# The sample's weighted expert rows: one DVE operation, or a scaling on ACT and an addition on POOL, in a hybrid decoder step

## The chip, the cores and the metric

The kernel runs on one core of a Trainium2 chip. A core has several engines that work side by side, each in the order of its own queue: TensorE (PE, matrix products; its weight loads are listed as PEld), VectorE (DVE), ScalarE (ACT) and GpSimd (POOL). SyncE (SP) and the other queues issue DMA transfers. The metric is the device time of one execution in microseconds (us), as the median of several runs. The kernel before has a median of 2448.68 us in three runs (2442.91 to 2449.34).

## The reference

The program is one inference step of a one-layer decoder, for a prompt of 512 tokens and for a sample group of 8 sequences of 8 tokens. Both go through a combined projection, a retention branch, a dilated-attention branch and a PEER block, with layer norms between. The PEER block is the part that matters here. It has 16,384 experts, each a row of two tables, `u_tab` and `v_tab`, of 1024 numbers. For each token and each of 8 heads it picks 16 experts by product keys and adds their rows up:

```python
def block(xb):
    q = (xb @ w_q).reshape(PEER_BLOCK, H_PEER, 2, DK_PEER // 2)
    s = jnp.einsum('thsc,hskc->thsk', q, sub_keys).astype(jnp.float32)
    sv, si = lax.top_k(s, TOPK_PEER)
    cand = (sv[:, :, 0, :, None] + sv[:, :, 1, None, :]).reshape(PEER_BLOCK, H_PEER, TOPK_PEER * TOPK_PEER)
    cv, ci = lax.top_k(cand, TOPK_PEER)
    i0 = jnp.take_along_axis(si[:, :, 0], ci // TOPK_PEER, axis=-1)
    i1 = jnp.take_along_axis(si[:, :, 1], ci % TOPK_PEER, axis=-1)
    e = i0 * N_KEYS + i1
    g = jax.nn.softmax(cv, axis=-1)
    a = jax.nn.gelu(jnp.einsum('td,thkd->thk', xb, u_tab[e]), approximate=False)
    return jnp.einsum('thk,thkd->td', (g * a).astype(xb.dtype), v_tab[e])
```

The last line is a weighted sum of rows. For the sample's 64 tokens the kernel computes it row by row.

## The kernel before, in words

All operations are emitted by one long function. A scheduler then orders the instructions of each engine by a simulation of the timeline, so the order in the code sets priorities and dependences, and not the order on an engine.

**The sample's experts.** The sample's 64 tokens lie twice on the 128 partitions, so that each partition sums half of a token's 128 experts: 64 steps. A step gathers one row of a table per partition into the tile `row` (128x1024 fp32) by an indirect DMA that POOL issues (`gather`, L1112); `row` has four buffers. `experts` first takes 64 rows of the u table (`dot`, L1121: a product with the token and its sum, on DVE), and then 64 rows of the v table (`add`). Of the v rows the first is multiplied by its weight (L1128); each of the others is one DVE operation that multiplies the row by its weight, a column of `a`, and adds it to the sum `ys` (L1130). `advance(n, after)` paces this: it first emits the operations of the rows that were asked for before (`consume`), then makes POOL copy one element of a tile named by `after` (L1144, tile `pace`), and lets n gathers follow that copy. So rows are asked for where the program around has got to a certain tile.

**The stage around the change.** By now 26 of the 64 v rows have been gathered. The prompt's routing begins, in four parts:

- *The scores.* For each of four column groups c, the projections by `w_q` run on PE, in eight accumulations per group, 32 in all, and ACT moves each from PSUM to the tile `qT` (L1463). `advance(GQ, ...)` with GQ = 4 stands twice in each group: eight requests of four rows, 32 rows. Then PE multiplies with the keys, ACT moves the scores to `sc` (L1470, three buffers), and DVE picks the 16 best of each 128 by maxima, index searches and replacements (`top16`, L991 to L999). Weights are split into a high and a low part: ACT copies (`whi`, L315), DVE subtracts (`wlo`, L316).
- *The head of the u-parts.* `u_ahead(HEAD)` runs 16 blocks of the dense expert product (`u_part`): ACT copies the weight (L1434), POOL subtracts for the low part (L1435), PE runs 24 matmuls into `tr` (L423 to L425), and ACT applies Gelu into `act` (L1440).
- *The spread.* `spread(t)`, for three tiles of 128 tokens. `route` combines the two key lists on DVE: candidate sums `cand` (L1013, L1015), their `top16`, a subtraction `ce` (L1030) whose exponential is taken by ACT (L1031), two chains of `eq` that pick the indices (to L1040), and the weights `gw` (L1044). PE transposes the indices and the weights (L1490) and ACT moves them to `tT` (L1492). Then 32 groups of four tokens each follow: one-hot matrices from DVE (`oh1` L1501, `oh0` L1511), ACT (L1507, L1508) and POOL (L1511), products of the two on PE (L1512), and ACT moves them to `stage` (L1513). After every fourth group stand one further `u_part` and `advance(GX, ...)` with GX = 1: six of the v rows fall here.
- *The rest.* The routing of the fourth tile, and 12 or so further u-parts before the main loop.

The main loop runs 128 blocks of the dense experts over some 840 us. In it the sample's result is finished and the fourth prompt tile goes through `experts` too, with 128 rows of each table.

Of the kernel before, what the change touches and what calls it, by code (L numbers as in the profile page):

```python
# [13 lines left out]
AF = mybir.ActivationFunctionType  # L14
OP = mybir.AluOpType
# [209 lines left out]
def body(tc, I, O, dbg=None):  # L225
    nc = tc.nc
    PE, DVE, ACT, POOL, SP = nc.tensor, nc.vector, nc.scalar, nc.gpsimd, nc.sync
# [9 lines left out]
    def pool(name, side=None, space=None):  # L237
        kw = {"reuse_waits": "tile"} if space is None else {"space": space}
        if side:
            kw["side"] = side  # L240
        return tc.alloc_tile_pool(name=name, bufs=1, **kw)
# [20 lines left out]
    def ac_ps():  # L262
        return psum("ac", 3)
# [106 lines left out]
    raws, units, state = [], [], {"done": 0, "bank": ac_ps, "ada": None}  # L370
# [38 lines left out]
    def take(name, c, u, n=2):  # L409

        a = state["done"]
        while len(units) < len(order) and sum(not plain(i) for i in range(a, len(units))) < UB:
            load_units()
            if len(units) == len(raws):
                break
            split_unit()
        load_units()
        assert order[a:a + n] == [(name, c, u + i) for i in range(n)] and len(units) >= a + n, (order[a], name, c, u)
        state["done"] += n
        return units[a:a + n]  # L420
# [120 lines left out]
    def proj_t(w, m, x, ks=range(8), sel=slice(0, L)):  # L541

        ps = mm_ps()[:, 0:sel.stop - sel.start]
        for k in ks:
            mm3(ps, both(w, k, slice(128 * m, 128 * m + 128)), x(k, sel), k == ks[0], k == ks[-1])
        return ps
# [441 lines left out]
    def top16(xs, vs, ixs):  # L988

        for x, v, ix in zip(xs, vs, ixs):  # L990
            DVE.max(v[:, 0:8], x)  # L991
        for x, v, ix in zip(xs, vs, ixs):
            DVE.max_index(ix[:, 0:8], v[:, 0:8], x)
        for x, v, ix in zip(xs, vs, ixs):
            DVE.match_replace(x, v[:, 0:8], x, MINF)
        for x, v, ix in zip(xs, vs, ixs):
            DVE.max(v[:, 8:16], x)
        for x, v, ix in zip(xs, vs, ixs):
            DVE.max_index(ix[:, 8:16], v[:, 8:16], x)  # L999
# [70 lines left out]
    def values(g):  # L1070
        v = two_blocks() + two_blocks()
        for half in range(2):
            w = take("w_av", g, 2 * half)
            cs = slice(256 * half, 256 * half + 256)
            for c in range(4):
                ACT.activation(v[c][:, cs], proj_n(w, h, tiles[c]), AF.Copy)  # L1076
        return v
# [22 lines left out]
    ys = S2.tile([128, D], F32, name="ys", tag="ys")  # L1100

    pending = []

    def consume():
        with tc.issue_after(state["split"]):
            for f in pending:
                f()
        pending.clear()

    def gather(table, e, j):  # L1110
        r = S2.tile([128, D], F32, name="row", tag="row", bufs=ROWS)
        POOL.indirect_dma_start(out=r, out_offset=None, in_=I[table], in_offset=bass.IndirectOffsetOnAxis(ap=e[:, j:j + 1], axis=0))  # L1112
        return r

    def experts(n, e, g, h2, y):

        a = S2.tile([128, 128], F32, name="acts", tag="acts", bufs=1)
        DVE.memset(a, 0.0)

        def dot(u, j):  # L1120
            DVE.scalar_tensor_tensor(u, u, 1.0, h2, op0=OP.mult, op1=OP.mult, accum_out=a[:, j:j + 1])  # L1121
            if j == n - 1:
                ACT.activation(a[:, 0:n], a[:, 0:n], AF.Gelu)
                DVE.tensor_tensor(a[:, 0:n], a[:, 0:n], g, op=OP.mult)

        def add(v, j):
            if j == 0:
                DVE.tensor_scalar(y, v, a[:, 0:1], None, op0=OP.mult)  # L1128
            else:
                DVE.scalar_tensor_tensor(y, v, a[:, j:j + 1], y, op0=OP.mult, op1=OP.add)  # L1130

        for f, table in ((dot, "u"), (add, "v")):
            for j in range(n):
                r = gather(table, e, j)
                pending.append(lambda f=f, r=r, j=j: f(r, j))
                yield
# [3 lines left out]
    def advance(n, after, steps=sample_steps):  # L1140

        consume()
        t = P0.tile([1, 1], F32, name="pace", tag="pace", bufs=2)
        with tc.issue_after(POOL.tensor_copy(t, after[0:1, 0:1]).ins):  # L1144
            for _ in range(n):
                next(steps, None)
# [55 lines left out]
    for g in range(NG):  # L1202
        v = v0 if g == 0 else values(g)
# [248 lines left out]
    sv = [C.tile([128, 16, 16], F32, name=f"sv{t}") for t in range(NT)]  # L1452
    si = [C.tile([128, 16, 16], U32, name=f"si{t}") for t in range(NT)]
    C1 = pool("scores", side="right")
    for c in range(4):
        keys = C1.tile([128, 4, 128], F32, name="keys", tag="keys", bufs=2)
        SP.dma_start(keys, I["keysT"][:, 4 * c:4 * c + 4, :])
        qT = C1.tile([128, 4, L], F32, name="qT", tag="qT", bufs=2)
        for a in range(2):
            ws = take("w_q", c, 2 * a)  # L1460
            for hv in (slice(0, 256), slice(256, 512)):
                for i in range(2):
                    ACT.activation(qT[:, 2 * a + i, hv], proj_t(ws[i:i + 1], 0, h2p, sel=hv), AF.Copy)  # L1463
            advance(GQ, qT[:, 2 * a])
        for t in range(NT):
            ps = ac_ps()
            for m in range(4):
                PE.matmul(ps[:, 128 * m:128 * m + 128], qT[:, m, tiles[t]], keys[:, m, :], start=True, stop=True)
            s = C1.tile([128, 4, 128], F32, name="sc", tag="sc", bufs=3)
            ACT.activation(s, c4(ps), AF.Copy)  # L1470
            cs = range(4 * c, 4 * c + 4)
            top16([s[:, m, :] for m in range(4)], [sv[t][:, i, :] for i in cs], [si[t][:, i, :] for i in cs])
    C1.release()
    C2 = pool("spread", side="right")
# [80 lines left out]
    def gathered():  # L1555
        yield from sample_steps
        consume()
        yc = M.tile([128, D], F32, name="yc", tag="pz", bufs=3)[0:NS]
        ACT.activation(yc, ys[NS:128, :], AF.Copy)
        DVE.tensor_tensor(yc, yc, ys[0:NS, :], op=OP.add)  # L1560
        gt2s = bcast(M, "gt2s", modD, 3072, NS, tag="x1", bufs=3)
        finish(0, [yc[:, 0:512], yc[:, 512:1024]], gt2s, O["y_s"].rearrange("b t d -> (b t) d"))
        y3 = S2.tile([128, D], F32, name="y3", tag="ys")
        yield from experts(128, e3, g3, h2g, y3)
        consume()
        finish(NT, [y3[:, 0:512], y3[:, 512:1024]], gt2, O["y_p"][0, 128 * TD:])

    steps = gathered()
    yps = [mm_ps(), mm_ps(), sp_ps(), ac_ps(), ac_ps(), ac_ps()]

# [35 lines left out]
    for i in range(128):  # L1606
# [4 lines left out]
        if i in actD:  # L1611
            a = ACTP.tile([128, ND], F32, name="act", tag="act", bufs=4)
            SP.dma_start(a, actD[i])
        else:
            a = u_part(i)
# [41 lines left out]
```

## Time and profile before

| | value |
|---|---|
| median of three runs | 2448.68 us (2442.91 to 2449.34) |
| profiled run | 2440.74 us |
| its span, first to last instruction | 2439.0 us |
| granted clock of TensorE, mean | 0.949 of full |
| PE busy | 2229.5 us, 91%, 12729 instructions |
| DVE busy | 1726.5 us, 71%, 3069 |
| ACT busy | 1008.4 us, 41%, 1663 |
| POOL busy | 1170.1 us, 48%, 982 |
| DMA | 677.56 MB, mean 278 GB/s |

The profile is of one execution, whose time stands in the second line. The first part of its page gives the busy time of each engine; the second cuts the span into 40 slices of 61 us, where a digit is the busy share in tenths. A row of a timeline gives the start, the duration, the engine, the line, the operation and its tiles (out<-in), and in brackets how long the engine had been idle and what ended that.

### The profile page before, as it was taken

The page shows a single profiled execution, that of the slowest core. Times are in us where ns is not written, and L with a number is a line of the kernel's source. Part 1 is how long each engine was busy: PE and PEld are TensorE (multiplying, and loading weights), DVE is VectorE, ACT ScalarE, POOL GpSimd, SP SyncE. Part 2 cuts the span into 40 slices and gives each one's busy share as a digit, 9 for nine tenths or more (in the row PEclk, how much of TensorE's full clock was granted, in tenths as well). Part 3 has the DMA queues.
Part 4 walks back from the last instruction along what each step waited for, and adds up shares of the span by engine and source line. Part 5 has one row for each costly group of instructions (what it writes and reads, how often), then busy time and mean ns, then how long its engine had stood idle before and what let it go on. Part 6 is the DMA issues. An engine that isn't in the chain of part 4 may idle for free.

```text
span 2439.0 us, 35771 instructions
## 1 busy us (share of the span) xinstructions
PE 2229.5 (91%) x12729; PEld 1885.9 (77%) x12729; DVE 1726.5 (71%) x3069; ACT 1008.4 (41%) x1663; POOL 1170.1 (48%) x982
## 2 busy tenths in 40 slices
PE   6899999968989997999889999989999999999994
PEld 3786666656877875899889999878888888888874
DVE  3563121254678788879999992488888788888887
ACT  2461222234446553233358895333333333333332
POOL 1113111043125654323566564676666667767773
PEclk7999999988989997999989999999999999999997
DMA  9686876468858998486767778789999999999982
GB/s 314 216 292 211 321 284 218 157 202 286 276 212 278 332 366 299 148 280 227 281 212 290 277 275 276 240 294 328 331 342 344 338 325 326 326 334 343 324 304 81
DMA packets 221438, 677.56 MB, mean 278 GB/s; under 512 B 28947, under 2 KB 78227, under 8 KB 217771
## 3 DMA queue, kind: packets, MB, share of 16 engines
q1 hardware_dynamic: 148960, 432.91, 51.3%
q0 software_dynamic: 63392, 228.31, 26.4%
q10 hardware_dynamic: 8908, 14.06, 1.6%
q8 instruction: 100, 1.64, 0.3%
q14 instruction: 78, 0.64, 0.1%
HBM read 617.40 MB, written 115.55 MB: 301 GB/s over the span
## 4 chain that ended last, share of the span: by engine, by line
PE 34%; DVE 23%; DMA 10%; issue 6%; POOL 3%; ACT 2%; SPq 0%; POOLq 0%; DVEq 0%; ACTq 0%
PE mm L423 4%; PE mm L425 4%; PE mm L424 4%; PE tr L425 3%; PE tr L423 3%; PE tr L424 3%; DVE wlo L316 2%; DVE ys L1130 2%; PE ac L425 2%; PE ac L424 2%; PE ac L423 2%; DMA act<-act 2%; DMA row<-in_u_dram,e 2%; DVE oh L1511 2%; DMA row<-in_v_dram,e 1%
## 5 line engine op out<-in xcount | busy, mean ns | idle before, releaser
L316 DVE TENSOR_TENSOR wlo<-wraw,whi 128x1024 fp32r<-128x1024 f32 x304 | 396.7, 1311 | 310.7 <-ACT whi L315 291.2
L315 ACT ACTIVATE whi<-wraw 128x1024 fp32r<-128x1024 f32 x304 | 319.4, 1057 | 449.1 <-PE mm L424 164.2
L1435 POOL TENSOR_TENSOR wlo<-wraw,whi 128x1024 fp32r<-128x1024 f32 x128 | 326.3, 2551 | 140.6 <-ACT whi L1434 131.1
L423 PE MATMUL tr<-x,whi 128*128 128x384 f32 x1024 | 351.4, 343 | 28.6 <-ACT whi L1434 14.7
L425 PE MATMUL tr<-x,wlo 128*128 128x384 f32 x1024 | 349.8, 342 | 1.9 <-POOL wlo L1435 1.8
L424 PE MATMUL tr<-x,whi 128*128 128x384 f32 x1024 | 349.6, 341 | 0.0
L1112 POOL DMA_INDIRECT row<-in_v_dram,e x192 | 241.2, 1256 | 173.7 <-DVE y L1130 70.1
L1112 POOL DMA_INDIRECT row<-in_u_dram,e x192 | 242.4, 1263 | 150.2 <-DVE row L1121 120.8
L423 PEld LDWEIGHTS tr<-x,whi 128*128 128x128 f32 x1024 | 195.3, 191 | 38.4 <-ACT whi L1434 19.8
L425 PEld LDWEIGHTS tr<-x,wlo 128*128 128x128 f32 x1024 | 195.1, 191 | 4.0 <-POOL wlo L1435 2.8
L424 PEld LDWEIGHTS tr<-x,whi 128*128 128x128 f32 x1024 | 194.9, 190 | 1.8
L1130 DVE SCALAR_TENSOR_TENSOR y<-row,acts,y 128x1024 f32<-128x1024 f32 x127 | 184.0, 1449 | 10.9 <-DMA row<-in_v_dram,e 9.7
L1121 DVE SCALAR_TENSOR_TENSOR row<-row,h2g 128x1024 f32<-128x1024 f32 x128 | 178.5, 1410 | 11.9 <-DMA row<-in_u_dram,e 11.7
L1434 ACT ACTIVATE whi<-wraw 128x1024 fp32r<-128x1024 f32 x128 | 135.0, 1055 | 113.7 <-PE ac L425 37.6
L423 PE MATMUL mm<-xh,whi 128*128 128x512 f32 x384 | 154.3, 402 | 0.8 <-ACT wraw L1076 0.4
L425 PE MATMUL mm<-xh,wlo 128*128 128x512 f32 x384 | 152.6, 398 | 0.0
L424 PE MATMUL ac<-wlo,wh 128*128 128x512 f32 x384 | 152.3, 397 | 0.0
L424 PE MATMUL mm<-xl,whi 128*128 128x512 f32 x384 | 151.9, 396 | 0.0
L423 PE MATMUL ac<-whi,wh 128*128 128x512 f32 x384 | 150.3, 397 | 0.0
L423 PE MATMUL mm<-whi,xh 128*128 128x256 f32 x448 | 134.1, 301 | 15.5 <-ACT xh L1092 5.8
L315 ACT ACTIVATE wh<-wt 128x384 fp32r<-128x384 f32 x128 | 66.1, 523 | 181.7 <-DVE wt L1578 180.8
L425 PE MATMUL ac<-whi,wl 128*128 128x512 f32 x384 | 139.8, 395 | 0.0
(418 smaller groups left out, 5343.8 us busy)
## 6 DMA issues: line engine op xcount, KB each, us to landing
wraw<-in_uT_dram SPq DMA_DIRECT2D x128, 512.0 KB
wraw<-in_v_dram SPq DMA_DIRECT2D x128, 512.0 KB
out_dram<-in_cache_dram SPq DMA_DIRECT2D x64, 508.0 KB
wraw<-in_w_ada_dram SPq DMA_DIRECT2D x48, 512.0 KB
act<-act SPq DMA_DIRECT2D x128, 192.0 KB
gate<-stage SPq DMA_DIRECT2D x12, 2048.0 KB
gt<-gate SPq DMA_DIRECT2D x191, 128.0 KB
kt<-in_kc_dram POOLq DMA_DIRECT2D x32, 588.0 KB, 5.6
```

What stands on the lines that cost most here:

```text
L315: ACT.activation(hi, src, AF.Copy)
L316: return DVE.tensor_tensor(lo, src, fv(hi), op=OP.subtract).ins
L423: PE.matmul(ps, a[0], b[0], start=first, stop=False)
L424: PE.matmul(ps, a[0], b[1], start=False, stop=False)
L425: PE.matmul(ps, a[1], b[0], start=False, stop=last)
L1112: POOL.indirect_dma_start(out=r, out_offset=None, in_=I[table], in_offset=bass.IndirectOffsetOnAxis(ap=e[:, j:j + 1], axis=0))
L1121: DVE.scalar_tensor_tensor(u, u, 1.0, h2, op0=OP.mult, op1=OP.mult, accum_out=a[:, j:j + 1])
L1130: DVE.scalar_tensor_tensor(y, v, a[:, j:j + 1], y, op0=OP.mult, op1=OP.add)
L1434: ACT.activation(uh, u, AF.Copy)
L1435: POOL.tensor_tensor(ul, u, fv(uh), op=OP.subtract)
L1511: E.tensor_scalar(oh0[:, j, :], num, col(0), col(2), op0=OP.is_equal, op1=OP.mult)
```

## The change

It adds a switch, `state["adder"]`. It stands on DVE until the scores pool has been made, on POOL during the scores and the spread, and on DVE again from the main loop on. While it stands on POOL, `add` emits two operations per row: ACT scales the row in its own buffer by the column of `a`, and POOL adds it to the sum. A further `consume()` stands ahead of the switch. It concerns 38 of the sample's 64 v rows; the fourth prompt tile's 128 rows stay with DVE.

```diff
--- before.py
+++ after.py
@@ -1100,6 +1100,7 @@
     ys = S2.tile([128, D], F32, name="ys", tag="ys")
 
     pending = []
+    state["adder"] = DVE
 
     def consume():
         with tc.issue_after(state["split"]):
@@ -1126,8 +1127,11 @@
         def add(v, j):
             if j == 0:
                 DVE.tensor_scalar(y, v, a[:, 0:1], None, op0=OP.mult)
+            elif state["adder"] is DVE:
+                DVE.scalar_tensor_tensor(y, v, a[:, j:j + 1], y, op0=OP.mult, op1=OP.add)
             else:
-                DVE.scalar_tensor_tensor(y, v, a[:, j:j + 1], y, op0=OP.mult, op1=OP.add)
+                ACT.activation(v, v, AF.Copy, scale=a[:, j:j + 1])
+                POOL.tensor_tensor(y, y, v, op=OP.add)
 
         for f, table in ((dot, "u"), (add, "v")):
             for j in range(n):
@@ -1452,6 +1456,8 @@
     sv = [C.tile([128, 16, 16], F32, name=f"sv{t}") for t in range(NT)]
     si = [C.tile([128, 16, 16], U32, name=f"si{t}") for t in range(NT)]
     C1 = pool("scores", side="right")
+    consume()
+    state["adder"] = POOL
     for c in range(4):
         keys = C1.tile([128, 4, 128], F32, name="keys", tag="keys", bufs=2)
         SP.dma_start(keys, I["keysT"][:, 4 * c:4 * c + 4, :])
@@ -1565,6 +1571,7 @@
         consume()
         finish(NT, [y3[:, 0:512], y3[:, 512:1024]], gt2, O["y_p"][0, 128 * TD:])
 
+    state["adder"] = DVE
     steps = gathered()
     yps = [mm_ps(), mm_ps(), sp_ps(), ac_ps(), ac_ps(), ac_ps()]
```

In the new file the lines from L1103 on are one further, those from L1131 on four, those from L1456 on six and those from L1568 on seven.

The scheduler gives each engine another order from the scores on. On POOL, at the start of the scores, the order before is a pacing copy and then four gathers (`row<-in_v_dram`), and so on:

```order
L1144 COPY pace<-z 1x1 x4
L1144 COPY pace<-qT 1x1
L1112 DMA row<-in_v_dram,e_5661 128x1024 x4
L1144 COPY pace<-qT 1x1
L1112 DMA row<-in_v_dram,e_5661 128x1024 x4
L1144 COPY pace<-qT 1x1
L1112 DMA row<-in_v_dram,e_5661 128x1024 x4
```

Now additions to `ys` stand among the gathers:

```order
L1148 COPY pace<-z 1x1 x4
L1148 COPY pace<-qT 1x1
L1113 DMA row<-in_v_dram,e_5661 128x1024 x4
L1134 TENSOR_TENSOR ys<-ys,row 128x1024 x3
L1148 COPY pace<-qT 1x1
L1113 DMA row<-in_v_dram,e_5661 128x1024 x2
L1134 TENSOR_TENSOR ys<-ys,row 128x1024
L1113 DMA row<-in_v_dram,e_5661 128x1024 x2
L1134 TENSOR_TENSOR ys<-ys,row 128x1024 x3
L1148 COPY pace<-qT 1x1
```

Three of the first four additions stand ahead of the next pacing copy, and from the second request on the gathers come in pairs or one by one, with additions between.

On ACT, at the same place (`qT<-mm` is the move of a finished projection, `whi` and `x` are splits of weights and of the stacked input), the order before is:

```order
L1463 ACTIVATE qT<-mm 128x256 x2
L315 ACTIVATE x_8491<-tr 128x4x128
L315 ACTIVATE x_8492<-tr 128x4x128
L315 ACTIVATE whi<-wraw 128x1024
L1463 ACTIVATE qT<-mm 128x256
L315 ACTIVATE whi<-wraw 128x1024
L1463 ACTIVATE qT<-mm 128x256 x3
L315 ACTIVATE whi<-wraw 128x1024
L1463 ACTIVATE qT<-mm 128x256
```

Now scalings of rows stand between them:

```order
L1469 ACTIVATE qT<-mm 128x256 x2
L315 ACTIVATE x_8491<-tr 128x4x128
L315 ACTIVATE x_8492<-tr 128x4x128
L1133 ACTIVATE row<-row,acts 128x1024 x2
L315 ACTIVATE whi<-wraw 128x1024
L1469 ACTIVATE qT<-mm 128x256
L1133 ACTIVATE row<-row,acts 128x1024 x2
L315 ACTIVATE whi<-wraw 128x1024
L1469 ACTIVATE qT<-mm 128x256 x3
L315 ACTIVATE whi<-wraw 128x1024
L1469 ACTIVATE qT<-mm 128x256
L1133 ACTIVATE row<-row,acts 128x1024 x2
```

The first two scalings have come to stand behind the second move, two more behind the third, and the fifth and sixth behind the seventh; further on the 24th stands behind the 26th, and the 28th behind the last.

On DVE, at the place where the first one-hot of the spread stands (`oh<-sp,tT`, of the first tile), the order before is the end of the second tile's candidates and its subtraction `ce`, and then the one-hots:

```order
L997 MAX cv<-cand 128x8 x8
L999 MAX_INDEX ci<-cv,cand 128x8 x8
L1030 TENSOR_TENSOR ce<-cv 128x128
L1501 TENSOR_TENSOR oh_11337<-sp,tT 128x512
L1511 TENSOR_SCALAR oh_11338<-sp,tT 128x128 x2
L1501 TENSOR_TENSOR oh_11351<-sp,tT 128x512
L1511 TENSOR_SCALAR oh_11352<-sp,tT 128x128 x3
```

Now the subtraction is followed by the rest of the second tile's routing, up to `gw` and the second index `i`, and by the candidates of the third tile:

```order
L999 MAX_INDEX ci<-cv,cand 128x8 x8
L1030 TENSOR_TENSOR ce<-cv 128x128
L1021 TENSOR_SCALAR ci<-ci 128x128
...
L1038 TENSOR_TENSOR eq<-eq 128x128x2
L1040 TENSOR_TENSOR i_12148<-eq 128x128
L1013 TENSOR_TENSOR cand<-sv_9192 128x8x64
L1015 TENSOR_TENSOR cand<-sv_9192 128x8x48
L991 MAX cv<-cand 128x8 x8
L993 MAX_INDEX ci<-cv,cand 128x8 x8
L995 MATCH_REPLACE cand<-cv,cand 128x112 x7
L1507 TENSOR_TENSOR oh_11365<-sp,tT 128x512
L1517 TENSOR_SCALAR oh_11366<-sp,tT 128x128 x2
```

The lines left out between the first piece and the last are the second tile's `cf` and `eq` operations. So the first one-hot has moved behind a part of two further tiles' routing; the 22 and 11 additions L1130 that stood ahead of it are gone from DVE.

## Rows read from the trace of the kernel before

**Rows 1.** The page's slices: busy tenths of PE and DVE in 40 slices.

```profile
PE   6899999968989997999889999989999999999994
...
DVE  3563121254678788879999992488888788888887
```

**Rows 2.** Windows by stage: window, length, then PE, PEld, DVE, ACT, POOL busy (instructions).

```profile
1054.00:1156.00 102.00, 101.85 (x843) 101.61 (x843) 90.17 (x348) 33.10 (x59) 32.35 (x35) 0.98 0.75 252
1156.00:1256.00 100.00, 79.03 (x429) 77.23 (x428) 99.62 (x372) 33.18 (x51) 59.53 (x27) 0.91 0.71 247
1256.00:1436.00 180.00, 173.13 (x1155) 169.42 (x1155) 179.37 (x457) 157.33 (x275) 113.68 (x83) 0.97 0.77 277
1436.00:1490.00 54.00, 54.00 (x381) 53.82 (x381) 38.02 (x89) 47.25 (x85) 29.15 (x25) 1.00 0.68 241
1490.00:1560.00 70.00, 66.42 (x367) 64.59 (x365) 6.18 (x6) 27.04 (x37) 33.72 (x15) 0.98 0.86 279
```

**Rows 3.** Groups by line, 1050 to 1510 us: busy us, mean ns; idle before.

```profile
L1130 DVE SCALAR_TENSOR_TENSOR ys<-row,acts,ys 128x1024 f32<-128x1024 f32 x38 | 60.0, 1580 | 0.1
...
L1435 POOL TENSOR_TENSOR wlo<-wraw,whi 128x1024 fp32r<-128x1024 f32 x55 | 144.9, 2636 | 95.9 <-ACT whi L1434 87.9 <-PE ac L1512 6.1 <-PE tr L425 0.8
...
L1434 ACT ACTIVATE whi<-wraw 128x1024 fp32r<-128x1024 f32 x55 | 58.0, 1054 | 37.8 <-PE tr L424 22.3 <-POOL wlo L1435 7.2 <-PE mm L424 3.3
```

**Rows 4.** The additions of line L1130 on DVE by stage (window, length, busy).

```profile
1054.00:1156.00 102.00, 30.50 (x22) 0.98 0.75 252
...
1156.00:1256.00 100.00, 20.03 (x11) 0.91 0.71 247
...
1256.00:1490.00 234.00, 9.50 (x6) 0.98 0.75 269
```

**Rows 5.** Timelines of POOL and DVE: two-operand work side by side and alone.

```profile
1180.02 2.41 POOL L1435 TENSOR_TENSOR wlo<-wraw,whi 128x1024 fp32r<-128x1024 f32 x1
...
1181.29 2.23 DVE L1130 SCALAR_TENSOR_TENSOR ys<-row,acts,ys 128x1024 f32<-128x1024 f32 x1
...
1211.93 1.27 DVE L1130 SCALAR_TENSOR_TENSOR ys<-row,acts,ys 128x1024 f32<-128x1024 f32 x1
...
1222.69 2.46 DVE L1044 TENSOR_TENSOR gw<-cv,rsm 128x128 f32<-128x128 f32 x1
...
1261.02 0.29 DVE L1044 TENSOR_TENSOR gw<-cv,rsm 128x128 f32<-128x128 f32 x1
```

**Rows 6.** Timelines of PE and DVE in the head, up to the first one-hot.

```profile
1222.39 0.69 PE L423 MATMUL tr<-x,whi 128*128 128x384 f32 x1 [9.33 <-ACT act L1440]
...
1244.96 0.33 PE L1490 MATMUL tr<-kc_ident,i 128*128 128x128 f32 x1 [4.19 <-DVE i L1040]
...
1218.98 0.27 DVE L1030 TENSOR_TENSOR ce<-cv 128x128 f32<-128x128 f32 x1
...
1244.94 0.69 DVE L1013 TENSOR_TENSOR cand<-sv 128x512 f32<-128x512 f32 x1
...
1255.02 0.69 DVE L1501 TENSOR_TENSOR oh<-sp,tT 128x512 f32<-128x512 f32 x1
```

**Rows 7.** Timeline of ACT: two of its waits for DVE.

```profile
1163.02 0.60 ACT L1470 ACTIVATE sc<-ac 128x512 f32<-128x512 f32 x1 [6.39 <-DVE si L999]
...
1219.28 0.31 ACT L1031 ACTIVATE cv<-ce 128x128 f32<-128x128 f32 x1 [11.89 <-DVE ce L1030]
```

**Rows 8.** Timeline of POOL in the scores, and the gathers' landing (count, us).

```profile
1052.21 1.00 POOL L1144 COPY pace<-qT 1x1 f32<-1x1 f32 x1 [1.84 <-ACT qT L1463]
...
1054.68 0.94 POOL L1112 DMA_INDIRECT row<-in_v_dram,e  x1 [0.30 <-issue]
...
1055.92 0.94 POOL L1112 DMA_INDIRECT row<-in_v_dram,e  x1 [0.30 <-issue]
...
1147.25 1.19 POOL L1144 COPY pace<-qT 1x1 f32<-1x1 f32 x1
...
row<-in_v_dram,e POOLq DMA_INDIRECT x32, 5.3
```

## The prediction

> **What bounds the kernel now.** I read the page's slices first, then the windows by stage, then the groups by line, then the timelines of the engines around the place of the change. The slices [rows 1] show TensorE at nine tenths or more over most of the span, so a change on DVE, ACT and POOL can only matter where PE has holes. The stage table [rows 2] cuts the stretch that the change touches. The scores (1054 to 1156 us) are PE-bound: 101.85 of 102 us busy, DVE 90.17. In the head of the u-parts (1156 to 1256) PE is busy for 79.03 of 100 us and DVE for 99.62: here DVE's routing chain is the limit, because the first transposes of the spread need its indices. In the first part of the spread (1256 to 1436) DVE is busy for 179.37 of 180 us and PE for 173.13; in its last part (1436 to 1490) PE is busy all the time. Behind that DVE has 6.18 of 70 us, so the change ends there.
>
> The two largest holes of PE in the head are plain in the timelines [rows 6]: 9.33 us before a u-part at 1222, and 4.19 us before the first transpose of the routing indices at 1245. The first comes by way of ACT: its exponential of the routing weights stands in order ahead of the Gelu that frees PE's next PSUM buffer, and waits 11.89 us for DVE's subtraction [rows 7]. The second ends with DVE's last index sum. Both are DVE being late.
>
> **How much there is to win.** By PE's own rate: the stretch after the spread runs 367 matmuls in 66.42 us of busy time, 0.181 us each [rows 2]. At that the head's 429 would take 77.6 us, so 22 us of its 100 are waits. The spread's last part runs 381 matmuls in 54 us, 0.142 us each; by that the first part's 1155 take 164 us of 180, another 16. That is 38 us at most, if PE were never kept waiting.
>
> **What is removed.** 38 of DVE's weighted adds, 60.0 us in all [rows 3]: 22 in the scores (30.50 us), 11 in the head (20.03), and the rest, 9.50, in the spread [rows 4].
>
> **What is added.** 38 scalings on ACT and 38 additions on POOL, neither of which the trace has on these tiles. The scaling is an ACT copy of 128x1024 fp32: the nearest row is whi's, 1054 ns [rows 3], 40 us in all. ACT is busy for a third of the scores and of the head [rows 2], so the time itself is covered there; what is not is the wait for the row's transfer, because ACT runs in order. The addition is a two-input POOL operation of 128x1024: wlo's is the nearest row, 2636 ns on the mean [rows 3] and 2.41 us undisturbed [rows 5]; I take 2.41, so 92 us in all. POOL has 70 us free in the scores and 40 in the head [rows 2].
>
> **The scores: the new loop.** Per request for the next rows POOL had one pacing copy and four gathers; now four additions stand among them. The gathers start 1.24 us apart at best (1054.68, 1055.92), so four rows cost 4 x (1.24 + 2.41) = 14.6 us on POOL, beside the pacing copy. Before, the first and the eighth pacing copy of the q tiles started at 1052.21 and 1147.25, 13.6 us apart on the mean [rows 8]. So POOL goes from a third busy to more than full, without any wait counted. And waits there are: a row takes 5.3 us to land [rows 8], then 1.05 us on ACT, and only four buffers carry the rows. On ACT the scalings now stand between the evacuations of the q projections: the first two behind the second evacuation, the fifth and sixth behind the seventh, the 24th behind the 26th, the 28th behind the last. A scaling that waits for its row holds up the evacuations behind it, and with them PE's PSUM buffers. Below, nothing is lost (PE stays the bound, the order leaves a slack of some three evacuations, or 10 us); above, each of eight requests takes 1.0 us more on POOL and half a microsecond for a landing: 12 us. A gain is excluded, since PE is full. I take 5.
>
> **The head: DVE's chain up to the first one-hot,** which started at 1255.02 [rows 6]. Out of it go the head's 20.0 us of adds, and the backlog that DVE brought in from the scores: at 1163 ACT had waited 6.39 us for DVE to free a scores buffer [rows 7]. With 30.5 of its 90.17 us gone DVE brings none; I put the backlog at 6 to 14 us and take 10. But the scheduler puts other work in the gap: what was left of the second tile's routing (its two index chains), and the third tile's candidates, now stand ahead of the first one-hot. The first tile's chain from its subtraction (1218.98) to its last index (1244.94) took 26 us beside POOL's subtractions [rows 6]; I count 20 for the second tile's, between a half of 26 and all of it. From the second tile's candidate sums (1244.94) to the first one-hot (1255.02) went 10 us [rows 6]; some two thirds of such a piece are pulled ahead for the third tile, 6.5 us (4 to 8). So the first one-hot moves by -20.0 - 10 + 20 + 6.5 = -3.5 us, between -16 and +8, and the scores' 5 us come on top: +1.5.
>
> **The spread.** DVE is freed of 9.5 us of adds and of the 26.5 us that were pulled ahead, out of 217.4 us (179.37 + 38.02 [rows 2]). PE then sets the pace, down to its 0.142 us a matmul: at most -16. ACT (157.33 of 180 us) gets 6 scalings, and POOL as many additions, so I don't count on all of it: -8, between -15 and 0. The stages behind only shift.
>
> **Sum:** +5 - 3.5 - 8 = -6.5 us. The profiled run took 2440.74 us (span 2439.0, 1.7 us around it), so such a run comes to 2434.2. The three timed runs have a median of 2448.68, 7.9 us above the profiled one; from there the forecast is 2448.7 - 6.5, some 2442 us. On this kernel 0.3% (7.3 us) is about what can be told from no change.
>
> **What speaks against it in the rows.** A DVE add that lay beside a POOL subtraction (which started at 1180.02 and took 2.41 us) took 2.23 us instead of 1.27, and the small product gw 2.46 instead of 0.29 [rows 5]. So a POOL operation with two SBUF operands holds up a DVE operation with two of them, by up to its own length. The routing has some 18 such DVE operations a tile. The Trainium skill says the same in "SBUF — State Buffer", section "Who interferes with whom": DVE's second operand comes through an interface that it shares with GpSimd, and the later of the two waits for the whole of the other; the trace agrees. "Perfetto Trace Analysis" in the Trainium skill, section "Optimizing Scalar/DVE Operations", warns for that reason that moving work from one of the two to the other might not help. What the mechanism does to the sum is the third rival.
>
> **Rivals.**
> 1. The relief passes through. DVE's chain gets shorter by its 50 us of adds in the scores and the head, the pulled work costs nothing since it had to be done by the later tiles anyway, and PE runs at its own rate. For it: DVE ends both holes. Against: the order above, and POOL's load. -31 us, between -25 and -37: 2418.
> 2. POOL becomes the bound of the scores: 14.6 us per four rows, a pacing copy, and 2 us of waiting for landings. ACT stands before a scaling whose row is late, the evacuation behind it waits, and PE stops. It decides from the point at which a row lands later than the evacuations ahead of its scaling are done, about 10 us after the pacing copy. Price 7 x 3 = +21 in the scores; the head gives nothing, the spread 7 back: +14, 2463. For it: POOL's sum is already over the pace. Against: the additions may slide into the head, where POOL has room.
> 3. No net change, because POOL's additions hold up the routing. POOL's busy share in the head goes from 60% to some 80%, so a fifth more of the 18 operations a tile would be caught, each losing about half of 2.41 us: 4 us a tile, 8 for the two tiles ahead of the first one-hot. The sum is +1.5: 2450.
>
> **Chances.** Forecast 0.42 (own range 2434 to 2449), rival 1 0.20, rival 2 0.20, rival 3 0.18. Faster by over 0.3% (below 2441): a little over half of the forecast and all of rival 1, 0.44. Slower by over 0.3%: rival 2 and a quarter of rival 3, 0.25. The rest, 0.31, lies within. The range goes from 2420 (over half of rival 1 left out) to 2463 (half of rival 2 left out).
>
> **What would show it.** Right: PE's 102 us for the scores grow by 0 to 12 us and POOL is nine tenths busy there; PE's wait for the Gelu is below 9 us; the first one-hot is at 1247 to 1263; DVE has idle time in the spread, and PE's 1155 matmuls take some 170 us. Rival 1 shows as a first one-hot before 1240. Rival 2 shows as PE waiting for ACT's evacuations in the scores, and ACT for transfers of rows or for POOL. Rival 3 shows as index operations of 2 us and more throughout the routing. Wrong altogether would be a difference outside of 1054 to 1490 us.

## The result and the profile after

The changed kernel is slower: 2456.59 us in the median of 14 runs (2450.87 to 2468.43) against 2442.65 for the kernel before (14 runs, 2435.74 to 2452.07), a ratio of 1.006 with an interval of 1.0043 to 1.0077, some 14 us. The profiled run is one of the longer ones, 2464.68 us, 24 us above the profiled run of before, so the stages below add up to more than the medians differ by.

I cut both traces at the same events: the start of the first evacuation of a q projection, the end of the 32nd, the start of the first one-hot, the end of the last one-hot product (each is the start, or start plus duration, of a row of the timelines). In us:

| | before | after | predicted change | measured |
|---|---|---|---|---|
| first evacuation starts at | 1051.7 | 1054.3 | | +2.6 |
| scores (to the end of the 32nd) | 104.9 | 114.3 | +5 | +9.4 |
| head (to the first one-hot) | 98.4 | 107.7 | -3.5 | +9.3 |
| spread (to the last product) | 233.9 | 235.3 | -8 | +1.4 |
| the rest | 950.1 | 951.3 | 0 | +1.2 |

The windows of these three stages in the changed kernel, in the columns of [rows 2], and then the scores of the kernel before, between the same events:

```profile
1054.00:1168.60 114.60, 107.03 (x850) 105.70 (x851) 84.35 (x402) 63.31 (x91) 104.13 (x65) 0.96 0.71 243
1168.60:1276.30 107.70, 79.67 (x427) 78.12 (x425) 106.39 (x350) 41.24 (x59) 74.59 (x32) 0.88 0.67 225
1276.30:1511.60 235.30, 227.28 (x1535) 223.26 (x1536) 191.86 (x478) 205.47 (x360) 147.83 (x113) 0.98 0.74 263
```

```profile
1051.70:1156.60 104.90, 103.13 (x852) 102.80 (x852) 92.85 (x352) 34.37 (x63) 34.59 (x36) 0.98 0.74 246
```

POOL (the fifth busy time) is as full in the scores as was forecast, 104.13 of 114.6 us. PE runs 852 matmuls in the scores before and 850 now, but needs 9 us more for them. In the spread DVE's busy time has fallen to 191.86 us and PE's has not: 227.28.

The new operations cost a little more than the prediction took for them (1149 ns a scaling for 1054, 2538 ns an addition for 2410), by line (columns as in [rows 3]):

```profile
L1439 POOL TENSOR_TENSOR wlo<-wraw,whi 128x1024 fp32r<-128x1024 f32 x53 | 135.8, 2566 | 91.3 <-ACT whi L1438 88.2 <-PE ac L1518 2.9
L1134 POOL TENSOR_TENSOR ys<-ys,row 128x1024 f32<-128x1024 f32 x38 | 96.4, 2538 | 4.4 <-ACT row L1133 3.7
...
L1133 ACT ACTIVATE row<-row,acts 128x1024 f32<-128x1024 f32 x38 | 43.6, 1149 | 27.5 <-DMA row<-in_v_dram,e 27.3
```

The last row holds the first loss: ACT stood idle for 27.3 us ahead of its scalings, for transfers of rows, 24.1 of them in the scores. A second hole stands in ACT's timeline in the head:

```profile
1228.16 0.47 ACT L1444 ACTIVATE act<-tr 128x384 f32<-128x384 f32 x1
1228.66 1.28 ACT L1031 ACT_TABLE_LOAD   x1
1246.13 0.31 ACT L1031 ACTIVATE cv<-ce 128x128 f32<-128x128 f32 x1 [16.19 <-DVE ce L1030]
1246.35 1.04 ACT L1438 ACTIVATE whi<-wraw 128x1024 fp32r<-128x1024 f32 x1
...
1261.48 0.48 ACT L1498 ACTIVATE tT<-tr 128x384 f32<-128x384 f32 x1
```

This exponential belongs to the second tile. In the kernel before it stands behind the move to `tT`, and waits 6.88 us there; now it stands ahead of four weight copies, of the Gelus between them and of `tT`, and it waits 16.19 us for a subtraction that DVE reaches at 1245.83. PE's row of the same moment, and DVE's three rows that bound it:

```profile
1249.24 0.69 PE L423 MATMUL tr<-x,whi 128*128 128x384 f32 x1 [13.64 <-ACT act L1444]
```

```profile
1235.51 0.39 DVE L1040 TENSOR_TENSOR i<-eq 128x128 f32<-128x128 bf16 x1
...
1245.83 0.27 DVE L1030 TENSOR_TENSOR ce<-cv 128x128 f32<-128x128 f32 x1
...
1276.28 0.69 DVE L1507 TENSOR_TENSOR oh<-sp,tT 128x512 f32<-128x512 f32 x1
```

The reader is to see two things. DVE had the first tile's last index at 1235.9, 9 us earlier than before (1244.9 [rows 6]) although the scores had ended 12 us later: the relief of DVE was there. And the first one-hot came 40 us behind this index, but not because it waited for ACT. `tT`, which it reads, was late (1261.48, before 1245.44), yet it was there 14.8 us before the one-hot started, and DVE was busy for 106.39 of the head's 107.70 us. DVE spent the 40 us on its own work: 10 us on the second tile's candidates, as before, and 30 us on further work for the next two tiles, from `ce` to the first one-hot. In the kernel before the one-hot follows `ce` at once.

Nor is a hole behind an exponential new: the kernel before has one of 9.3 us, behind the first tile's [rows 6, rows 7]. PE's waits in its head (total, times, longest, in us):

```profile
PE tr L423 <- ACT act L1440: 13.1, 3, 9.3
PE tr L1490 <- DVE i L1040: 4.2, 1, 4.2
PE ac L1512 <- ACT oh L1508: 3.7, 1, 3.7
```

These are 21.0 us; the changed kernel's, shown further on, are 28.8.

### The profile page after: what moved, and what is told of

It is laid out like the page before. It is cut to its first block, busy times and chain, and to the rows that moved or that the text cites. A ratio compares the mean times of both kernels' runs of the same rounds, so it can differ in the third digit from the quotient of the medians.

```text
span 2462.9 us, 35808 instructions
## 1 busy us (share of the span) xinstructions
PE 2229.7 (91%) x12729; PEld 1883.3 (76%) x12729; DVE 1698.7 (69%) x3031; ACT 1047.3 (43%) x1701; POOL 1270.5 (52%) x1020
## 4 chain that ended last, share of the span: by engine, by line
PE 57%; DVE 15%; DMA 14%; issue 5%; POOL 4%; ACT 3%; SPq 1%; POOLq 0%; ACTq 0%; DVEq 0%
PE mm L423 8%; PE mm L425 7%; PE mm L424 7%; PE tr L423 4%; PE tr L425 4%; PE tr L424 4%; DMA act<-act 3%; PE ac L1518 3%; PE ac L425 2%; PE ac L748 2%; PE ac L424 2%; PE ac L423 2%; DMA row<-in_v_dram,e 2%; DVE wlo L316 2%; DMA vecD<-vt 2%
## 5 line engine op out<-in xcount | busy, mean ns | idle before, releaser
L1131 DVE SCALAR_TENSOR_TENSOR y<-row,acts,y 128x1024 f32<-128x1024 f32 x127 | 186.4, 1467 | 11.6 <-DMA row<-in_v_dram,e 10.7
```

## The experiments

All are timed against the kernel before on the same chip; the times of stages are from one profile each. My theory after the comparison: the scores lose to waits, the head to the order of instructions, and the spread is PE's and has nothing to win.

**Where it is lost.** The first run sets the switch behind the scores only.

```diff
     C1 = pool("scores", side="right")
-    consume()
-    state["adder"] = POOL
...
     C1.release()
+    consume()
+    state["adder"] = POOL
     C2 = pool("spread", side="right")
```

> The switch is set to POOL only behind the scores, so the six rows of the spread go to ACT and POOL and the 32 others stay on DVE. Theory (scores and instruction order cost all): scores and head as before (last qT within 1 us, first one-hot 1254 to 1257 us), ratio 0.998 to 1.002. Rival (POOL's additions in the spread hold up DVE's one-hots and ACT's stage): the spread's 234 us grow by 3 or more, ratio above 1.002.

Measured: ratio 1.0015 (0.9998 to 1.0031). Scores 104.9 us, as before; first one-hot at 1252.5, earlier than expected. Up to there the code is that of before, ACT's order is the same and only DVE's differs in places, and still the head took 94.6 us instead of 98.4: a difference of this size in the head says little. The spread took 240.7 us in this profile, so the rival cannot be excluded for its six rows; the ratio leaves at most 0.3% to them. The scores and the head hold the bulk of the loss.

**The order.** Two kernels keep everything of the change and only constrain the order. The first queues each exponential behind the preceding tile's `tT`; the second also queues DVE's work behind `ce` behind the third one-hot group.

```diff
-        ACT.activation(cv, ce, AF.Exp)
+        with (tc.issue_after(after) if after else contextlib.nullcontext()): ACT.activation(cv, ce, AF.Exp)
...
-        route(C, 8, sv[t], si[t], i01, g)
+        route(C, 8, sv[t], si[t], i01, g, state.get("tT"))
...
-        ACT.activation(tT[:, 3, :], pt[:, 256:384], AF.Copy, scale=-1.0)
+        state["tT"] = ACT.activation(tT[:, 3, :], pt[:, 256:384], AF.Copy, scale=-1.0).ins
```

> The changed kernel, with one constraint: ACT's exponential of the second tile's routing (and of the third) is queued behind the move of the preceding tile's indices to tT, as in the order of the kernel before. Theory (the order on ACT costs what the head lost): the 16.19 us wait of ACT before that exponential goes, PE's 13.64 us hole with it, the first tT is at 1245 to 1250 us instead of 1261.5; DVE's pulled routing still stands ahead of the first one-hot, so that one comes at 1268 to 1274. Ratio to before 1.001 to 1.005. Rival (POOL in the scores costs everything, the order nothing): ratio 1.004 to 1.008 as for the changed kernel.

Measured: 1.0041 (1.0022 to 1.0059), which lies in the ranges of the theory and of the rival, so the times must decide. `tT` comes 76.1 us behind the last evacuation instead of 92.9, the first one-hot 99.5 instead of 107.7. (On the clock these are 1236.2 and 1259.6, earlier than expected; in this profile the scores began 8 us earlier.) PE's waits from the end of the scores into the first one-hots:

```profile
PE ac L1518 <- DVE oh L1507: 19.1, 2, 18.6
PE tr L423 <- ACT act L1444: 6.6, 3, 3.7
```

PE's hole of 13.64 us is gone, and PE waits for the one-hots instead. So the theory holds only in part: the exponential's place cost PE the hole, but DVE's pulled work is what holds the one-hot, here as in the changed kernel. It is shorter here (16.1 us from `ce` to the one-hot instead of 30.5), because the scheduler now leaves most of the third tile's candidates behind the one-hot and fewer of the operations come out long.

```diff
+        with (tc.issue_after(state["oh"]) if after else contextlib.nullcontext()):
             DVE.tensor_scalar(ci[:, 0], ci[:, 2], 4, None, op0=OP.logical_shift_right)
...
-                DVE.tensor_tensor(oh1, iota_p[:, None, :].to_broadcast(sh), ...)
+                ins = DVE.tensor_tensor(oh1, iota_p[:, None, :].to_broadcast(sh), ...)
+                if b == 0 and q == 2: state["oh"] = ins.ins
```

> As the one before, and in addition DVE's work on the next tile's routing, from behind its subtraction, is queued behind the third one-hot group of the tile before. Theory (order alone undid the relief in the head): first one-hot at 1245 to 1252 us, against 1276 in the changed kernel and 1255 before; the scores keep their 9 us of loss. Ratio to before 0.995 to 1.000. Rival (the scores' loss is what counts and the spread is limited by DVE, so that the routing that returns to it costs as much there): ratio 1.002 to 1.006.

Measured: 0.9991 (0.9976 to 1.0007). The first one-hot comes 85.3 us behind the last evacuation, 22 us earlier than in the changed kernel and 13 earlier than before. PE's waits between the scores and the one-hots (total, times, longest, in us) in the changed kernel, and with both constraints:

```profile
PE tr L423 <- ACT act L1444: 19.2, 4, 13.6
PE ac L1518 <- DVE oh L1507: 9.6, 1, 9.6
```

```profile
PE tr L423 <- ACT act L1445: 5.7, 3, 3.5
PE ac L1520 <- ACT oh L1516: 5.0, 1, 5.0
```

The intervals of the changed kernel and of this one lie apart: order alone was worth some 0.7%, all of the loss. The scores' loss is still in it (112.8 us): by stage its profile has 7.9 us more than before in the scores, 13.1 less in the head, 5.2 less in the spread and 6.8 more behind it.

**The scores: POOL or ACT?** One kernel gives the additions back to DVE and leaves ACT's scalings; another, with both constraints, leaves POOL's additions and takes out the scalings.

```diff
                 ACT.activation(v, v, AF.Copy, scale=a[:, j:j + 1])
-                POOL.tensor_tensor(y, y, v, op=OP.add)
+                DVE.tensor_tensor(y, y, v, op=OP.add)
```

> The changed kernel with the addition on DVE instead of POOL: ACT still scales each row in order. Theory (in the scores PE loses to ACT, which stands before scalings whose rows come late because POOL, full with additions, asks for them late): with POOL free the rows come in time and the scores last 102 to 104 us from first to last evacuation, against 114 in the changed kernel and 105 before. Rival (ACT's waiting for rows costs by itself, whoever adds): 110 us or more. DVE's addition of two SBUF tiles should take 1.2 to 1.4 us, so the head is as before: ratio 0.999 to 1.004.

Measured: 1.0007 (0.9989 to 1.0026). The scores took 113.4 us with POOL a third busy (34.50 of 106 us), so my theory of a full POOL falls: the rival holds. ACT waits for rows whoever adds them (here DVE is late in its turn, as two of the waits below show). The head took 89.8 us, 8.6 less than before, although it was expected to stay; scores and head together are as long as before (203.2 and 203.3 us).

```diff
-                ACT.activation(v, v, AF.Copy, scale=a[:, j:j + 1])
                 POOL.tensor_tensor(y, y, v, op=OP.add)
```

> The kernel with both constraints (exponential and routing held), without ACT's scaling of the 38 rows: POOL adds the rows unweighted, so the sample's result lacks their weights. Theory (ACT's waits for the rows, in order ahead of evacuations and weight copies, cost the scores; POOL being full does not): the 32 evacuations take 104 to 106 us as before, with POOL as full as in the changed kernel. Rival (POOL): 111 us or more. Ratio to before 0.992 to 0.998 by the theory, 0.998 to 1.001 by the rival.

Measured: 0.9988 (0.9963 to 1.0014). The scores took 106.4 us with POOL nearly full (the fifth busy time):

```profile
1054.00:1160.00 106.00, 101.69 (x837) 100.72 (x836) 88.27 (x401) 34.05 (x62) 97.56 (x60) 0.98 0.72 250
```

The mechanism is as the theory has it: 6.5 us of the scores come back. The total is not: it lies in the rival's range and can't be told from the 0.9991 with the scalings. So what the scores' loss is worth in the whole is not shown. A third kernel, with both constraints, keeps the scalings, but queues them on ACT behind the last evacuation of the next request, with three rows a request:

```diff
-        with tc.issue_after(state["split"]):
+        with tc.issue_after(state["split"]), (tc.issue_after(state["qT"]) if "qT" in state else contextlib.nullcontext()):
...
+            state["qT"] = q_ins
             advance(GQ, qT[:, 2 * a])
```

> With both constraints, the scalings queued on ACT behind the last evacuation of the request after theirs, and three rows a request instead of four (eight rows move to the main loop, where DVE adds them). Theory: a row has a whole request's 13.6 us to be asked for and to land, so ACT waits little for rows and the scores take 104 to 108 us; ratio 0.993 to 0.998. Rival (POOL's chain of gather, landing, scaling and addition is too long for the pace even with three): 110 us or more, ratio 0.998 or more.

Measured: scores 105.1 us, ratio 1.0018 (0.9994 to 1.0041). ACT's waits for rows in the scores, in the changed kernel, with DVE adding, and with the later scalings:

```profile
ACT row L1133 <- DMA row<-in_v_dram,e: 24.1, 17, 3.4
```

```profile
ACT row L1133 <- DMA row<-in_v_dram,e: 14.1, 7, 2.7
...
ACT row L1133 <- DVE sc L995: 8.0, 1, 8.0
...
ACT row L1133 <- DVE wlo L316: 3.3, 1, 3.3
```

```profile
ACT row L1134 <- DMA row<-in_v_dram,e: 1.5, 1, 1.5
```

Where ACT doesn't wait for rows, the scores take what they took before (here with 24 rows asked for in them instead of 32; the share of that was not separated). The total didn't follow: its spread took 257.6 us, with 14 of POOL's additions in it instead of six, and with 1584 matmuls instead of 1526, more than two u-parts of 24 matmuls' worth; what came behind was 8 us shorter.

**What the relief could be worth, and what POOL's reading costs.** Two kernels keep both constraints. One drops scaling and addition.

```diff
-                ACT.activation(v, v, AF.Copy, scale=a[:, j:j + 1])
-                POOL.tensor_tensor(y, y, v, op=OP.add)
+                pass
```

> The same kernel without scaling and without addition: the 38 rows are gathered and never used. It is the most that the relief of DVE can be worth. Theory (the spread is limited by PE, only the head has a hole that DVE ends): scores 104 to 106 us, first one-hot 80 to 86 us behind the last evacuation (98.4 before), the spread 229 to 234 us; ratio 0.991 to 0.996. Rival of the prediction (all relief passes through, 25 us and more): ratio 0.990 or less.

Measured: 0.9856 (0.9825 to 0.9886), 35 us; scores 103.9, head 73.1, spread 224.1. The ceiling of the first rival (25 to 37 us) is real, with the order held, and the theory's range was too small: more than a quarter of it comes from the spread. The other occupies POOL without reading anything from SBUF.

```diff
-                ACT.activation(v, v, AF.Copy, scale=a[:, j:j + 1])
-                POOL.tensor_tensor(y, y, v, op=OP.add)
+                POOL.memset(v, 0.0)
+                POOL.memset(v, 0.0)
```

> With both constraints, but instead of scaling and adding a row POOL fills its buffer with zeros twice: POOL is occupied at the same places and waits for the same rows, and reads no operand from SBUF; the 38 rows are lost to the sample's result. Theory (POOL's additions cost the routing by holding up DVE's two-operand work, up to their own length): the 23 two-operand DVE operations of the head take 27 to 36 us in all, as with no additions (34.3), and not 41 to 47 as with them; first one-hot 73 to 77 us behind the last evacuation; ratio 0.984 to 0.990. Rival (POOL's own queue, busy with additions, is late with the subtractions of the u-parts): first one-hot at 80 us or later and ratio 0.993 or more.

Measured: 0.9912 (0.9891 to 0.9933), just above the theory's range; head 73.0 us. DVE's subtractions for the weight splits in the scores (two SBUF operands, 12 of them) by line, in this order: before, changed, additions on DVE, additions on POOL alone, POOL filling with zeros.

```profile
L316 DVE TENSOR_TENSOR wlo<-wraw,whi 128x1024 fp32r<-128x1024 f32 x12 | 14.5, 1212 | 11.1 <-ACT whi L315 11.1
```

```profile
L316 DVE TENSOR_TENSOR wlo<-wraw,whi 128x1024 fp32r<-128x1024 f32 x12 | 24.5, 2045 | 21.0 <-ACT whi L315 21.0
```

```profile
L316 DVE TENSOR_TENSOR wlo<-wraw,whi 128x1024 fp32r<-128x1024 f32 x12 | 14.6, 1215 | 15.1 <-ACT whi L315 13.9 <-DMA wraw<-in_w_q_dram 1.2
```

```profile
L316 DVE TENSOR_TENSOR wlo<-wraw,whi 128x1024 fp32r<-128x1024 f32 x12 | 28.8, 2414 | 13.0 <-ACT whi L315 13.0
```

```profile
L316 DVE TENSOR_TENSOR wlo<-wraw,whi 128x1024 fp32r<-128x1024 f32 x12 | 14.8, 1232 | 22.7 <-ACT whi L315 22.7
```

The same in the head, for the index sums and the candidate sums: before, with both constraints, then with POOL filling with zeros.

```profile
L1038 DVE TENSOR_TENSOR eq<-eq 128x1024 bf16<-128x1024 bf16 (+2 forms) x6 | 9.3, 1547 | 0.1
...
L1015 DVE TENSOR_TENSOR cand<-sv 128x384 f32<-128x384 f32 x2 | 3.9, 1958 | 0.0
```

```profile
L1039 DVE TENSOR_TENSOR eq<-eq 128x1024 bf16<-128x1024 bf16 (+2 forms) x6 | 13.8, 2292 | 0.1
L1015 DVE TENSOR_TENSOR cand<-sv 128x384 f32<-128x384 f32 x2 | 8.4, 4210 | 0.0
```

```profile
L1039 DVE TENSOR_TENSOR eq<-eq 128x1024 bf16<-128x1024 bf16 (+2 forms) x6 | 7.3, 1214 | 0.1
...
L1015 DVE TENSOR_TENSOR cand<-sv 128x384 f32<-128x384 f32 x2 | 1.1, 565 | 0.0
```

And the last index of the first tile, by which DVE's chain in the head can be measured: with both constraints, without additions, with zeros.

```profile
1240.40 0.42 DVE L1041 TENSOR_TENSOR i<-eq 128x128 f32<-128x128 bf16 x1
```

```profile
1216.35 2.52 DVE L1041 TENSOR_TENSOR i<-eq 128x128 f32<-128x128 bf16 x1
```

```profile
1213.03 2.50 DVE L1041 TENSOR_TENSOR i<-eq 128x128 f32<-128x128 bf16 x1
```

These end 75.2, 61.0 and 60.8 us behind the last evacuation (71.2 with POOL's additions and no scalings, 88.3 before). So the third rival's mechanism is shown: it takes POOL's additions, not POOL's being busy. They keep 10 to 14 us of DVE's relief in the head from coming through. The eight operations alone lose 13.8 us by them (22.2 against 8.4); in the kernel before, where POOL's subtractions for the u-parts catch some of them, they took 13.2. "SBUF — State Buffer" in the Trainium skill, section "Who interferes with whom", makes the same distinction between a GpSimd operation that reads SBUF and one that only writes it; the trace agrees, with 1232 ns beside 2414. What costs this kernel the rest against the one without additions (0.9912 to 0.9856; two fillings take 1.91 us, an addition 2.54, and the spread is 6 us longer, with 4.7 us more of busy time on DVE for the same 540 instructions) stays open.

**Relief without POOL and ACT.** All additions stay on DVE, with both constraints and two rows a request, so that 16 rows come later; then the same without the constraints (the second is the kernel before with this one edit).

```diff
-GQ = 4
+GQ = 2
```

> All additions stay on DVE, as before; both constraints; two rows a request instead of four, so that 16 rows move to the main loop, where DVE has room. Theory (what the head needs is fewer additions on DVE, wherever they go): first one-hot 86 to 92 us behind the last evacuation, scores 104 to 106 us, ratio 0.993 to 0.998. Rival (the rows cost the main loop what the head gains, since the fourth tile's rows come later): ratio 0.999 to 1.003.

Measured: 2432.61 us, 0.9965 (0.9944 to 0.9986), with scores of 103.9 and 76.8 us to the first one-hot, less than the 86 to 92 that were expected: faster than both kernels, and the fastest complete version of this study. The expected place of the rows was wrong: 16 more additions lay in the spread, which took 256.4 us, and the work behind it was shorter by 8.6.

> The kernel before with two rows a request instead of four, all additions on DVE and no constraint on the order: DVE is relieved in the scores and the head, and the scheduler has put the second tile's exponential ahead of three u-parts and of tT again. Theory (the order takes the relief back, whatever gave it): 10 to 20 us worse in the head than the same kernel with the constraints (76.8 us to the first one-hot), ratio to before 0.999 to 1.005 against 0.9965. Rival (only POOL's and ACT's new work makes that order costly): ratio 0.995 to 0.998.

Measured: 1.0039 (1.0023 to 1.0055), 101.6 us to the first one-hot, with the same rows a request and the same engines. Its spread took 237.3 us with the same 22 additions in it. So the constraints made the head 24.8 us shorter and the spread 19.1 longer: there are 1580 matmuls in it with them and 1535 without, and DVE is busy for 248 of its 256 us with them. The medians keep 12 us of the gain. ACT's and PE's waits from the end of the scores on, in the kernel without constraints:

```profile
ACT cv L1031 <- DVE ce L1030: 18.6, 2, 13.5
```

```profile
PE tr L423 <- ACT act L1440: 16.4, 4, 10.9
PE ac L1512 <- DVE oh L1501: 9.4, 1, 9.4
```

These are the two holes of the changed kernel, without anything on POOL or ACT, and DVE again spends 29.4 us between the second tile's `ce` and the first one-hot. So a relief of DVE is enough to make the scheduler reorder, whatever gives it.

Two further kernels asked for no rows in the spread (`GX = 0`, with a rate of 3.2 rows a block in the main loop), with two rows a request and with one.

> All additions on DVE, both constraints, two rows a request in the scores and none asked for in the spread; 22 rows move behind the spread, and the main loop's rate is 3.2 rows a block instead of 3.0. With the constraints and two rows a request alone, 22 additions had landed in the spread, which took 256 us instead of 234. Theory: the spread takes 225 to 235 us, the head 75 to 79, ratio 0.988 to 0.994. Rival (what is won in the spread is lost behind it, since u-parts only change places): ratio 0.995 to 0.998.

> As the last, with one row a request in the scores, so that 30 rows move behind the spread. Theory (two rows already leave DVE no backlog into the head): like the last within 0.2%, head 71 to 76 us. Rival (the main loop's DVE is full enough that more rows there cost): 0.3% or more slower than the last.

Measured: 1.009 (1.0064 to 1.0116) and 1.0142 (1.0111 to 1.0173). Head and spread were as forecast (76.8 and 73.1; 225.0 in both), but the rest took 1000.4 and 1015.5 us instead of 950: both theories fall. From the first of the two to the second only eight more rows move, and the rest grows by 15 us, so the main loop has no room for them at this rate. How much of the 50 us before that is the rate, changed at the same time, was not separated.

## Why the prediction was wrong

The forecast of 2442 us, 6.5 below the median of before then known (2448.68; 14 runs put it at 2442.65), had the sign wrong: the change cost some 14 us.

**The head: the step that failed.** The prediction took the first one-hot for the end of DVE's chain. That held: DVE worked almost without a pause up to it. What failed is the sum for this chain, -3.5 us, which measured +9.3. (Its bounds add up to -17 and +8, not to -16 and +8, and the measured value lies beyond them.) The relief was put at 30 us, with nothing taken off for POOL's additions; what these do to DVE's two-operand operations was left to the third rival. Without additions the first tile's last index does come 27 us earlier behind the scores' end (88.3 to 61.0), so the relief as such was well judged. With them it came 21.0 us earlier in the changed kernel. The pulled work was seen, and put at 26.5 us; it took 30.5, of which 24.1 went to the second tile's chains (put at 20) and 6.3 to the third tile's candidates (put at 6.5). No addition ran on POOL by then (its last in the head started at 1219.5), but its subtractions for the u-parts did. The -21.0, and 30.5 in place of 0.2 us before, are the whole +9.3. That the order is the larger part is shown by the two constraints: with the pulled work held back the head is 22 us shorter (107.7 to 85.3). ACT's new order in the head, an exponential ahead of four weight copies and of `tT`, was not weighed at all; it cost PE a hole of 13.64 us, but it did not set the first one-hot as the engines ran.

**The scores.** The direction and the cause on ACT were right, the size of +5 was short of 9.4 and within the bounds of 0 to 12. The reason given first, POOL's 14.6 us per four rows against a pace of 13.6, is not it: POOL at 97.56 of 106 us cost 1.5 us, and ACT's scalings with POOL at 34.50 cost 8.5.

**The spread.** The -8 us came from a rate of 0.142 us a matmul, read from the spread's last part. PE reached it in the second half of the changed kernel's spread (829 matmuls in 117.6 us), but the first third was slower than before. The first thirds, before and after:

```profile
1255.00:1333.00 78.00, 73.58 (x478) 71.55 (x479) 78.00 (x196) 64.70 (x114) 51.58 (x39) 0.96 0.77 280
```

```profile
1276.30:1354.70 78.40, 71.70 (x454) 69.39 (x455) 78.33 (x222) 65.19 (x111) 60.62 (x42) 0.94 0.70 251
```

DVE is full there in both, though 26 us of its routing had been pulled ahead; its idle time, and PE's better rate, come only behind that, and make up for no more than the first third loses. Why the first third lost 24 matmuls stays open. The 224.1 us of the run without additions show that some 10 us can be had in the spread when POOL and ACT get no new work either; 14 matmuls fewer in the stage (1512 against 1526) are some 2 us of them.

**The rivals.** The second rival's +14 us is what was measured, and that is luck: it had +21 us in the scores, nothing in the head and -7 in the spread, where the profiles have +9.4, +9.3 and +1.4. Of its mechanism ACT's part is what the scores show, and POOL's is not. The first rival's 31 us is there if nothing replaces the additions and the order is held (35 us). The third had the contention right; its 8 us for the head compare with the 10 to 14 us at the last index and with the 9.0 us that the eight operations took beyond the kernel before.

## What to carry to other kernels

Where a scheduler sets the order, taking work off the bounding engine can change the order on every engine, its own included. Read the new order of the freed engine first: what now stands ahead of the instruction that the bound waits for. Then look on the others for an instruction that waits for a later tile and has moved ahead of work for this one. A hole that a trace shows need not be the limit: when it was closed here, the wait moved elsewhere. Moving work to an engine also moves its reads of SBUF; count what these do to the engine that was to be relieved in the sum, and not beside it. And a run that simply drops the moved work tells early whether the rest is worth an argument.

## What was not expected of the hardware

Filling 128x1024 fp32 with zeros took POOL 955 ns and left DVE's two-operand subtractions at 1232 ns, beside 1212 with no such work on POOL, while an addition of the same size took 2538 ns and brought them to 2045 and 2414 ns. The zeros were not free for DVE either: its second index searches in the scores took 329 ns, against 286 without additions. The granted clock of PE in the head fell from 0.91 to 0.88 with its longer holes. Behind the hole of 13.64 us it stood at 0.50, the lower of its two levels (1.2 of 2.4 GHz), for the first 5 us, with 15 matmuls in them, and at 0.98 in the next 5.8, with 34:

```profile
1249.20:1254.20 5.00, 4.96 (x15) 4.96 (x16) 5.00 (x4) 1.32 (x2) 4.97 (x2) 0.50 0.63 159
1254.20:1260.00 5.80, 5.80 (x34) 5.80 (x34) 5.70 (x9) 1.44 (x2) 2.40 (x1) 0.98 1.07 406
```
